# First inner-layer group split without waiting, sums moved behind emptied banks, in a two-layer hybrid decoder trunk

## The chip, the cores and the metric

One core of one Trainium2 chip runs the whole program. The metric is device time in microseconds (us) of one execution, the median of several. TensorE is called PE here, VectorE DVE, ScalarE ACT, GpSimd POOL; SP is the queue on which almost all DMAs are issued.

## The reference

256 tokens of width 1024 pass through two layers. Each layer has a block of token mixers and then a squared-ReLU MLP of inner width 4096; all that the change touches is the MLP:

```python
def squared_relu_mlp(h, w_up, w_down):
    return jnp.square(jax.nn.relu(h @ w_up)) @ w_down
...
    for l in range(DEPTH):
        ...
        h = rms_norm(x, mlp_norm[l])
        x = x + squared_relu_mlp(h, w_mlp_up[l], w_mlp_down[l])
    return rms_norm(x, final_norm)
```

Everything is float32, and the results are wanted at nearly float32 precision.

## The kernel before

**Three products for one.** Every float32 operand is split into a rounded part (`hi`, type fp32r) and the rest (`lo`). A product is three matmuls (`three`, lines 300 to 303): hi with hi, hi with lo, lo with hi. ACT makes `hi` by a copy, DVE makes `lo` by a subtraction. For a weight the copies are `whi<-raw` (L280) and `wlo<-raw,whi` (L282); for the inner activations they are `sq<-hturned` on ACT and on DVE (both L322).

**The stream of weights.** Weights come in pieces of 128 x 1024 floats, 512 KB, in the order of use. SP issues their DMAs (`raw<-wts`, L218) into 7 rotating `raw` buffers, and the split pieces go to 6 rotating `whi`/`wlo` pairs. A DMA can start when DVE has finished with the `raw` buffer that it overwrites, and a split when PE has finished with the pair that it overwrites. One piece is 12 matmuls for PE.

**The MLP.** `up(i)` multiplies by one piece of the first matrix, `down(i)` by one of the second. Four ups make a group `g` of 512 inner columns for 256 tokens, in two PSUM banks (`pup`, tag `misc`, four banks). `squared_relu(g)` then sends the group on a long way: ACT applies the relu (L1332) and squares (L1334), DVE transposes blocks of 32 (`hblocks`, L331), one DMA writes them to HBM (`bounce`, L343), four DMAs read them back so that the inner columns lie on the partitions (`hturned`, L347), and `h_ready(g)` splits the result into `sq` (L322). PE needs `sq` for the four downs of that group. The order of PE's work is written out by hand in `mlp_order`: ten ups first (`LEAD = 10`), then downs and ups in turn. So the first down of a layer comes six ups after the group that it needs is complete.

**Seven products for eight.** For the groups in `SEVEN`, 1, 2, 3, 4 and 6 of each layer, two of the four downs are replaced by `seven(f)`, a 2 x 2 block product with seven multiplications. It needs sums of blocks of the activations (`h_sums`: four DVE operations `hsum`, then a split into `sumhi`, `sumlo`) and sums of blocks of the weights (`wsum`, `raw<-wsum,raw`, each split likewise). Two of the seven products go into the two banks of the group `g + 2`, which are then added into SBUF tiles (`carried`, L1402). The next ups need these banks. The first time this is a copy, on ACT in the kernel before.

**What sets the order.** Instructions are recorded in program order and then ordered by a scheduler for each engine, except where the kernel pins them. Each engine works through its queue strictly in order. `behind[key]` lists instructions after which the DMA and the split of the weight `key` are to be placed, and `tc.issue_after(x)` places what follows after `x`. The list `order` holds the weights still to be fetched, so `order[4]` is the fifth from there. In the second layer DVE also makes `xblocks`, transposes of the residual stream, and SP issues the DMAs that belong to them (`xbounce`, `xtok`).

Of the kernel before, what the change touches and what calls it, by code (L numbers as in the profile page):

```python
# [21 lines left out]
NF = DFF // P  # L22
# [6 lines left out]
SEVEN = [(1, 2, 3, 4, 6)] * L  # L29
# [127 lines left out]
def trunk(ctx: ExitStack, tc: tile.TileContext, gx, wts, consts, gfin, gn, xtok, out):  # L157


    nc = tc.nc  # L160
# [166 lines left out]
    def blocks_tile(name):  # L327
        return sb.tile([P, 4 * S], F32, name=name + "blocks", tag="probT", bufs=2)
# [1 line left out]
    def turn_row(blocks, t, row):  # L330
        return nc.vector.transpose(blocks.rearrange("p (b j t e) -> p t j b e", b=4, j=4, t=2)[:, t], row)  # L331

    def turned_blocks(rows, name, tag, bufs):

        blocks = blocks_tile(name)
        for t in range(NT):
            turn_row(blocks, t, rows[t])
        return turned_by_hbm(blocks, name, tag, bufs)

    def turned_by_hbm(blocks, name, tag, bufs, last=None):  # L340

        bounce = dr.tile([P, 4 * S], F32, name="bounce", bufs=2)
        nc.sync.dma_start(bounce, blocks)  # L343
        turned = sb.tile([P, 4 * S], F32, name=name + "turned", tag=tag, bufs=bufs)
        for b in range(4):
            src = bounce.rearrange("(a p) (b r) -> b p a r", a=4, b=4)[b]
            dma = nc.sync.dma_start(turned[32 * b : 32 * b + 32, :].rearrange("p (a r) -> p a r", a=4), src)  # L347
        if last:
            behind.setdefault(last, []).append(dma)
        return turned  # L350
# [458 lines left out]
    def layer(l, xn, before):  # L809
# [219 lines left out]
        first = slot("mv", 3)  # L1029
# [28 lines left out]
        first = slot("gmoba1", 1)  # L1058
# [269 lines left out]
        def squared_relu(g):  # L1328

            rows = [w2k("relu") for _ in range(NT)]  # L1330
            for t in range(NT):
                relu = nc.scalar.activation(rows[t], us[g][t], AF.Relu, scale=xm.col[t])  # L1332
            for t in range(NT):
                nc.scalar.activation(rows[t], rows[t], AF.Square)  # L1334
            turned = turned_blocks(rows, "h", "t4", T4)
            if g + 1 < NF // 4:
                behind.setdefault(order[3 if g - 2 in SEVEN[l] else 4], []).append(relu)
            waiting[g] = turned
            if 0 < g < NF // 4 - 1:
                h_ready(g - 1, relu)  # L1340
            elif g:
                h_ready(g)

        waiting = {}

        def h_ready(g, after=None):

            turned = waiting.pop(g)
            sq = sb.tile([P, 2, 4, S], F32R, name="sq", tag=("Q", "KK")[g % 2], bufs=1)
            with ExitStack() as pinned:  # L1350
                if after:
                    pinned.enter_context(tc.issue_after(after.ins))
                latest[:] = split_turned(turned, [sq[:, i] for i in range(2)])
            for j in range(4):
                h2[4 * g + j] = sq[:, 0, j, :], sq[:, 1, j, :]
            if g in SEVEN[l]:
                sums[g] = h_sums(turned)

        sums, shared, carried = {}, [], []

# [13 lines left out]
        def seven(f):  # L1374

            g = f // 4
            first, final = g == SEVEN[l][0], g == SEVEN[l][-1]
            t1 = load_w(l, "down", f, 0)
            w11, t2, t3, t4, w21, w22 = load_w(l, "down", f + 1, 0)
            if first:  # L1380
                shared.extend(misc_tile(name) for name in ("pone", "pfive"))
                carried.extend(w2k("carried") for _ in range(NT))
            s1, s2, s2a, s3 = sums.pop(g)
            (a11, a12), a22 = ([tuple(h[:, :P] for h in h2[f + i]) for i in range(2)]), tuple(h[:, P:] for h in h2[f + 1])
            ends = dict(start=first, stop=final)
            middle = dict(start=False, stop=False)
            alone = dict(start=True, stop=True)
            moving = us.pop(g + 2, None) or [misc_tile("pend") for _ in range(NT)]
            for o, a, b, marks in (
                (shared[1], s1, t1, ends),  # L1390
                (accs[0], a12, w21, middle),
                (shared[0], a11, w11, ends),
                (accs[2], a22, t4, middle),
                (moving[1], s3, t3, alone),
                (moving[0], s2, t2, alone),
                (accs[1], s2a, w22, middle),
            ):
                three(o, *a, *b, **marks)
            emptied = []
            for i in (1, 0):  # L1400
                r, o = carried[i], moving[i]
                emptied.append(nc.scalar.copy(r, o) if first else nc.vector.tensor_add(r, r, o))  # L1402
            if final:
                shares()
            else:
                following = SEVEN[l][SEVEN[l].index(g) + 1]
                for key in (order[3], (l, "down", 4 * following + 2, 0)):
                    behind.setdefault(key, []).extend(emptied)

        def shares():  # L1410

# [34 lines left out]
        last = l == L - 1  # L1446
# [108 lines left out]
        for t in range(NT):  # L1555
            y = sb.tile([P, D], F32, name="y", tag="t4", bufs=T4)
            r = sb.tile([P, 1], F32, name="fr", tag="st", bufs=SMALL)
# [50 lines left out]
T4 = 8  # L1608
# [82 lines left out]
```

## Time and profile before

| quantity | value |
|---|---|
| median of the three runs | 813.55 us (813.05, 813.55, 817.36) |
| the profiled execution | 813.68 us |
| its span, first to last instruction | 811.8 us |
| mean granted clock of PE | 0.997 |
| PE busy | 800.5 us |
| DVE busy | 663.7 us |
| ACT busy | 480.3 us |
| read from and written to HBM | 168.81 MB, 18.87 MB |

A line of the timeline gives the start, the length, the engine, the line of the kernel, the operation, what it writes and reads, how many such in a row, and in brackets the idle time before it and what ended that. In the chain of waits each line is a start, a length and what the time went to; a DMA's length is that from its issue to its landing. The lines of the `windows` view give, for a stretch of time, the busy time of each engine and, after these, the granted PE clock. The lengths of the matmuls are modelled; their starts are recorded, so that the pace of PE is read from one start to the next.

### The profile page before, as it was taken

What the parts mean: (1) busy time and instruction counts of PE and PEld (TensorE: products, weight loads), DVE (VectorE), ACT (ScalarE), POOL (GpSimd) and SP (SyncE); (2) the same over time, 40 slices, a digit from 0 to 9 for tenths busy, and PEclk for the clock granted to TensorE, in tenths of its full rate; (3) what the DMA queues carried; (4) which work ended last, traced back from release to release, by engine and by line L of the source; (5) the groups of instructions that cost most, each with busy time, mean ns of one, the idle gap of its engine ahead of it and who ended that gap; (6) DMA issues with size and microseconds to landing.
All of it is one profiled execution on the core that took longest, in us unless ns stands there. A gap on an engine that the chain in (4) does not pass through costs nothing.

```text
span 811.8 us, 11411 instructions
## 1 busy us (share of the span) xinstructions
PE 800.5 (99%) x3921; PEld 666.5 (82%) x3921; DVE 663.7 (82%) x1128; ACT 480.3 (59%) x755; POOL 72.8 (9%) x63
## 2 busy tenths in 40 slices
PE   9999999999998999999999999999999999999997
PEld 7888887888887888888898888888888878788885
DVE  6869997978875878887797987698698757889786
ACT  7675664654565666666486566655545656666562
POOL 0100810000030000000025220000001200000000
PEclk9999999999999999999999999999999999999999
DMA  9975979965667767788647579689665587688851
GB/s 331 353 241 166 295 236 288 288 234 197 204 219 232 214 218 256 256 270 253 226 160 223 159 226 331 217 262 264 219 236 176 186 271 235 218 270 292 309 180 54
DMA packets 68122, 192.11 MB, mean 237 GB/s; under 512 B 8288, under 2 KB 25056, under 8 KB 67808
## 3 DMA queue, kind: packets, MB, share of 16 engines
q1 hardware_dynamic: 67488, 190.71, 72.4%
q8 instruction: 31, 0.51, 0.3%
q10 hardware_dynamic: 576, 0.67, 0.2%
q14 instruction: 27, 0.22, 0.1%
HBM read 168.81 MB, written 18.87 MB: 231 GB/s over the span
## 4 chain that ended last, share of the span: by engine, by line
PE 90%; DMA 3%; DVE 3%; ACT 1%; issue 1%; SPq 0%; POOL 0%; DVEq 0%; ACTq 0%
PE acc L301 17%; PE acc L303 17%; PE acc L302 16%; PE pup L301 6%; PE pup L302 6%; PE pup L303 6%; PE acc L1270 6%; PE acc L512 4%; PE acc L514 2%; DMA hturned<-bounce 1%; PE ps_s L1036 1%; DMA bounce<-hblocks 1%; DVE wlo L282 1%; PE acc L878 1%; PE po L675 1%; DMA raw<-wts 1%
## 5 line engine op out<-in xcount | busy, mean ns | idle before, releaser
L280 ACT ACTIVATE whi<-raw 128x1024 fp32r<-128x1024 f32 (+4 forms) x267 | 268.7, 1020 | 187.7 <-PE acc L303 107.5
L282 DVE TENSOR_TENSOR wlo<-raw,whi 128x1024 fp32r<-128x1024 f32 (+4 forms) x267 | 318.6, 1209 | 71.6 <-ACT whi L280 70.5
L301 PE MATMUL acc<-whi,xs 128*128 128x512 f32 (+1 forms) x304 | 119.4, 394 | 0.1
L302 PE MATMUL acc<-wlo,xs 128*128 128x512 f32 (+1 forms) x304 | 117.8, 388 | 0.0
L303 PE MATMUL acc<-whi,xs 128*128 128x512 f32 (+1 forms) x304 | 117.7, 388 | 0.0
L301 PE MATMUL pup<-whi,xs 128*128 128x512 f32 x256 | 99.8, 391 | 0.9 <-ACT carried L1402 0.9
L302 PE MATMUL pup<-wlo,xs 128*128 128x512 f32 x256 | 100.1, 391 | 0.0
L303 PE MATMUL pup<-whi,xs 128*128 128x512 f32 x256 | 99.7, 389 | 0.0
L301 PE MATMUL acc<-whi,sq 128*128 128x512 f32 x196 | 77.1, 394 | 2.0 <-ACT sq L322 2.0
L303 PE MATMUL acc<-whi,sq 128*128 128x512 f32 x196 | 77.0, 393 | 1.1 <-DVE sq L322 1.1
L302 PE MATMUL acc<-wlo,sq 128*128 128x512 f32 x196 | 76.8, 392 | 0.0
L301 PEld LDWEIGHTS acc<-whi,xs 128*128 128x128 f32 x304 | 57.0, 188 | 13.5 <-issue 0.8
L303 PEld LDWEIGHTS acc<-whi,xs 128*128 128x128 f32 x304 | 57.1, 188 | 11.4
L302 PEld LDWEIGHTS acc<-wlo,xs 128*128 128x128 f32 x304 | 57.1, 188 | 10.7
L301 PEld LDWEIGHTS pup<-whi,xs 128*128 128x128 f32 x256 | 48.1, 188 | 11.5 <-ACT carried L1402 1.3
L303 PEld LDWEIGHTS pup<-whi,xs 128*128 128x128 f32 x256 | 48.2, 188 | 10.1
L302 PEld LDWEIGHTS pup<-wlo,xs 128*128 128x128 f32 x256 | 48.2, 188 | 9.8
L603 ACT ACTIVATE prob<-prob,smx 128x128 f32<-128x128 f32 x64 | 28.3, 444 | 31.4 <-DVE smx L600 31.4
L388 POOL TENSOR_TENSOR sqsum<-sqsum,xsq 128x256 f32<-128x256 f32 x16 | 18.3, 1141 | 314.9 <-ACT xs L317 169.7
L301 PEld LDWEIGHTS acc<-whi,sq 128*128 128x128 f32 x196 | 36.9, 188 | 10.3 <-ACT sq L322 2.8
L303 PEld LDWEIGHTS acc<-whi,sq 128*128 128x128 f32 x196 | 37.1, 189 | 9.7 <-DVE sq L322 1.9
L302 PEld LDWEIGHTS acc<-wlo,sq 128*128 128x128 f32 x196 | 37.1, 189 | 7.7
(273 smaller groups left out, 1344.7 us busy)
## 6 DMA issues: line engine op xcount, KB each, us to landing
raw<-wts SPq DMA_DIRECT2D x264, 512.0 KB, 5.0
bounce<-hblocks SPq DMA_DIRECT2D x16, 512.0 KB, 4.5
hturned<-bounce SPq DMA_DIRECT2D x64, 128.0 KB, 3.7
pbounce<-blocks SPq DMA_DIRECT2D x8, 768.0 KB, 4.1
probT<-pbounce SPq DMA_DIRECT2D x32, 192.0 KB, 6.5
qkoth<-qkraw SPq DMA_DIRECT2D x48, 64.0 KB, 5.2
raw<-wts SPq DMA_DIRECT2D x5, 464.0 KB, 6.0
dec<-consts SPq DMA_DIRECT2D x2, 1024.0 KB, 7.0
```

The source lines that it names most:

```text
L280: fetched.append(nc.scalar.activation(hi[:, cs], raw[:, cs], AF.Copy))
L282: nc.vector.tensor_sub(lo[:, cs], raw[:, cs], hi[:, cs].bitcast(F32))
L301: nc.tensor.matmul(o, ah, bh, start=start, stop=False, **more)
L302: nc.tensor.matmul(o, ah, bl, start=False, stop=False, **more)
L303: nc.tensor.matmul(o, al, bh, start=False, stop=stop, **more)
L388: (nc.gpsimd if n < self.on_pool else nc.vector).tensor_add(self.sum, self.sum, sq)
L512: nc.tensor.matmul(acc, wh[:, k, :], xn.both(k), start=k == 0, stop=False)
L514: nc.tensor.matmul(acc[:, 0:S], wl[:, k, :], xn.k(k)[0], start=False, stop=k == KD - 1)
L603: nc.scalar.activation(p[:, a:b], p[:, a:b], AF.Exp, bias=m[:, 2 + i : 3 + i], scale=d**-0.5, accum_out=m[:, 4 + i : 5 + i])
L675: nc.tensor.matmul(dst, vh, pT[h + j][0], start=True, stop=False)
L878: nc.tensor.matmul(mq[n], wq[n][0], xn.both(k), start=k == 0, stop=False)
L1270: nc.tensor.matmul(o, a, b, start=half == 0 and i == 0, stop=4 * half + n == KD and i == len(jobs) - 1)
```

## The change

Five edits. First, `squared_relu(0)` of each layer calls `h_ready(0)` at once, where before the split of group 0 was made in `squared_relu(1)` and placed after the relu of group 1. Second, the weight of `down 4` is placed behind the last of the four reads of group 0. Third, for groups 0 to 2 no weight is placed behind the relu any more. Fourth, for a group in `SEVEN` whose predecessor is in it too (2, 3 and 4), the sums are no longer made in `h_ready` but at the end of the `seven` of the predecessor, after the last of the two instructions that empty its banks. Fifth, the first of these emptyings is a copy on DVE instead of ACT.

```diff
-    def turned_blocks(rows, name, tag, bufs):
+    def turned_blocks(rows, name, tag, bufs, last=None):
...
-        return turned_by_hbm(blocks, name, tag, bufs)
+        return turned_by_hbm(blocks, name, tag, bufs, last)
...
-            turned = turned_blocks(rows, "h", "t4", T4)
-            if g + 1 < NF // 4:
+            waiting[g] = turned_blocks(rows, "h", "t4", T4, None if g else (l, "down", 4, 0))
+            if SEVEN[l][0] <= g - 2 < NF // 4 - 3:
                 behind.setdefault(order[3 if g - 2 in SEVEN[l] else 4], []).append(relu)
-            waiting[g] = turned
-            if 0 < g < NF // 4 - 1:
+            if 1 < g < NF // 4 - 1:
                 h_ready(g - 1, relu)
-            elif g:
+            elif g != 1:
                 h_ready(g)
...
             if g in SEVEN[l]:
-                sums[g] = h_sums(turned)
+                if g - 1 in SEVEN[l]:
+                    waiting[g] = turned
+                else:
+                    sums[g] = h_sums(turned)
...
-                emptied.append(nc.scalar.copy(r, o) if first else nc.vector.tensor_add(r, r, o))
+                emptied.append(nc.vector.tensor_copy(r, o) if first else nc.vector.tensor_add(r, r, o))
...
+            if g + 1 in waiting and g + 1 in SEVEN[l]:
+                with tc.issue_after(emptied[-1].ins):
+                    sums[g + 1] = h_sums(waiting.pop(g + 1))
```

PE's own order is the same, matmul for matmul. On ACT, where the MLP begins (the same in both layers), the order before runs from the weight splits ahead of group 0's relu to group 0's split:

```order
L280 ACTIVATE whi<-raw 128x1024 x2
L1332 ACTIVATE relu<-pup,ms 128x512 x2
L280 ACTIVATE whi<-raw 128x1024
L1334 ACTIVATE relu<-relu 128x512 x2
L280 ACTIVATE whi<-raw 128x1024 x3
L1332 ACTIVATE relu<-pup,ms 128x512 x2
L280 ACTIVATE whi<-raw 128x1024
L1334 ACTIVATE relu<-relu 128x512 x2
L322 ACTIVATE sq<-hturned 128x1024
```

In this piece the first pair of relus is that of group 0, the second that of group 1. On ACT at the same place the order is now:

```order
L280 ACTIVATE whi<-raw 128x1024 x3
L1332 ACTIVATE relu<-pup,ms 128x512 x2
L1334 ACTIVATE relu<-relu 128x512 x2
L280 ACTIVATE whi<-raw 128x1024 x3
L322 ACTIVATE sq<-hturned 128x1024
L1332 ACTIVATE relu<-pup,ms 128x512 x2
L280 ACTIVATE whi<-raw 128x1024
L1334 ACTIVATE relu<-relu 128x512 x2
```

The weight split that stood between relu and squares has gone ahead of the relu, and group 0's split stands ahead of group 1's relu instead of behind its squares. On SP at the same place in the first layer, the difference between the two orders, minus for before and plus for now:

```order
 L343 DMA bounce<-hblocks 128x1024
+L218 DMA raw<-wts 128x1024
+L347 DMA hturned<-bounce 32x4x256 x4
+L218 DMA raw<-wts 128x1024 x3
+L343 DMA bounce<-hblocks 128x1024
 L218 DMA raw<-wts 128x1024 x2
 L347 DMA hturned<-bounce 32x4x256 x4
-L218 DMA raw<-wts 128x1024 x2
-L343 DMA bounce<-hblocks 128x1024
-L218 DMA raw<-wts 128x1024
-L347 DMA hturned<-bounce 32x4x256 x4
```

One weight, that of `down 4`, has moved from ahead of group 0's four reads to behind them, and one more weight stands ahead of group 1's reads. On DVE, in the second layer around the first `seven`, the order before from the weight sums ahead of group 2's split to the second half of group 3's block transposes:

```order
L241 TENSOR_TENSOR wsum<-raw 128x512 x2
L282 TENSOR_TENSOR wlo<-raw,whi 128x1024
L241 TENSOR_TENSOR wsum<-wsum,raw 128x512
L1367 TENSOR_TENSOR hsum<-hturned 128x128
L1368 TENSOR_TENSOR hsum<-hturned 128x128
L241 TENSOR_TENSOR raw<-wsum,raw 128x512
L1369 TENSOR_TENSOR hsum<-hsum,hturned 128x128
L322 TENSOR_TENSOR sq<-hturned,sq 128x1024
L1370 TENSOR_TENSOR hsum<-hsum,hturned 128x128
L331 STREAM_TRANSPOSE hblocks<-relu 128x4x4x32
```

Here the two copies `carried<-pup` are not in DVE's queue; they stand on ACT behind `sumhi<-hsum`. On DVE at the same place now, from group 2's split to the first two weight sums:

```order
L322 TENSOR_TENSOR sq<-hturned,sq 128x1024
L331 STREAM_TRANSPOSE hblocks<-relu 128x4x4x32
L1461 STREAM_TRANSPOSE xblocks<-GX 128x4x4x32
L1461 STREAM_TRANSPOSE xblocks<-x_70 128x4x4x32
L282 TENSOR_TENSOR wlo<-raw,whi 128x1024
L1404 COPY carried<-pup 128x512
L331 STREAM_TRANSPOSE hblocks<-relu 128x4x4x32
L1404 COPY carried<-pup 128x512
L1369 TENSOR_TENSOR hsum<-hturned 128x128
L1370 TENSOR_TENSOR hsum<-hturned 128x128
L241 TENSOR_TENSOR wsum<-raw 128x512 x2
```

The sums of group 2's activations and of the weights have moved behind the two copies, which are DVE's own now.

## The prediction

> **What bounds the kernel now.** I read the busy times first, then PE's waits, then the places where PE waited, and last the chain of waits that leads to each.
>
> ```profile
> span 811.8 us, 11411 instructions
> ...
> PE 800.5 (99%) x3921; PEld 666.5 (82%) x3921; DVE 663.7 (82%) x1128; ACT 480.3 (59%) x755; POOL 72.8 (9%) x63
> ```
>
> PE is busy in 99% of the span and does the same work after the change. So only time in which PE waits or runs slowly can be won. The view of PE's waits names three in the MLPs:
>
> ```profile
> PE acc L301 <- ACT sq L322: 2.0, 2, 1.5
> PE acc L303 <- DVE sq L322: 1.1, 2, 0.5
> PE pup L301 <- ACT carried L1402: 0.9, 1, 0.9
> ```
>
> Those are 4.0 us, but the columns (total, times, longest) do not hold all that a wait costs. In the first layer PE comes to group 0's first down at 256.7:
>
> ```profile
> 256.72 0.39 PE L303 MATMUL pup<-whi,xs 128*128 128x512 f32 x1
> 258.65 0.50 PE L301 MATMUL acc<-whi,sq 128*128 128x512 f32 x1 [1.54 <-ACT sq L322]
> ...
> 259.91 0.50 PE L303 MATMUL acc<-whi,sq 128*128 128x512 f32 x1 [0.52 <-DVE sq L322]
> ...
> 264.35 0.39 PE L303 MATMUL pup<-whi,xs 128*128 128x512 f32 x1
> 264.58 0.39 PE L301 MATMUL pup<-whi,xs 128*128 128x512 f32 x1
> ```
>
> At full pace one matmul follows another by 0.23 us (264.35 to 264.58). From 256.72 to 264.35 there are 15 steps, which should take 15 x 0.23 = 3.45 us and took 7.63: 4.2 us are lost, 2.06 in the two waits and most of the rest in the slow matmuls behind them. The stretches of the clock say why:
>
> ```profile
> 256.90:260.70 3.80, 1.74 (x6) 0.97 (x6) 2.07 (x2) 2.95 (x3) 0.00 (x0) 1.00 0.73 292
> 260.70:264.20 3.50, 3.50 (x10) 2.75 (x9) 1.43 (x2) 0.44 (x1) 0.00 (x0) 0.53 0.56 180
> ```
>
> After the waits the granted clock is 0.53 over 3.5 us, so 0.47 x 3.5 = 1.6 us go there. In the second layer the same place costs less, and the wait for `carried` comes in addition:
>
> ```profile
> 659.09 0.39 PE L303 MATMUL pup<-whi,xs 128*128 128x512 f32 x1
> ...
> 661.54 0.40 PE L301 MATMUL acc<-whi,sq 128*128 128x512 f32 x1
> ...
> 698.08 0.39 PE L303 MATMUL acc<-whi,sq 128*128 128x512 f32 x1
> 699.32 0.50 PE L301 MATMUL pup<-whi,xs 128*128 128x512 f32 x1 [0.86 <-ACT carried L1402]
> 699.66 0.39 PE L302 MATMUL pup<-wlo,xs 128*128 128x512 f32 x1
> ```
>
> Four steps from 659.09 to 661.54 took 2.45 instead of 0.92: 1.5 us. Two from 698.08 to 699.66 took 1.58 instead of 0.46: 1.1 us. So 4.2 + 1.5 + 1.1 = 6.8 us are what the change can win at these places.
>
> **Group 0: why it is late.** The chain of waits in the first layer:
>
> ```profile
> 241.31 1.27 ACT relu L1332 x2
> ...
> 243.56 1.07 DVE wlo L282
> ...
> 244.70 1.31 DVE hblocks L331 x2
> ...
> 246.03 3.88 DMA bounce<-hblocks
> ...
> 251.28 6.17 DMA hturned<-bounce
> ...
> 257.54 1.06 ACT sq L322
> ...
> 258.63 1.24 DVE sq L322
> ```
>
> ACT's split began when the last of the four reads landed, not when ACT was free. From its start to PE's first matmul are 258.65 - 257.54 = 1.11 us, and to the third, which needs DVE's part, 259.91 - 257.54 = 2.37. Without a wait PE would start these at 256.95 and 257.41. So ACT must start by 255.04 for PE not to wait at all: the split is 2.5 us late.
>
> *The weight split ahead of the relu.* It stood between relu and squares and held both ACT and DVE up.
>
> ```profile
> 237.84 1.06 ACT L280 ACTIVATE whi<-raw 128x1024 fp32r<-128x1024 f32 x1 [1.66 <-PE pup L303]
> ...
> 243.41 1.15 ACT L1334 ACTIVATE relu<-relu 128x512 f32<-128x512 f32 x2
> ```
>
> Weight splits wait for PE, which takes 12 x 0.23 = 2.76 us for a piece. So the next may start at 240.60 and end at 241.66. The relus then start 0.35 later than before and end at 242.93, the two squares end at 243.5 and 244.1, and DVE, done with the weight at 241.66 + 1.2 = 242.9, transposes each half as it comes, 0.65 each: the bounce is issued near 244.8 instead of 246.03, 1.2 us earlier.
>
> *One weight behind the reads.* SP's queue at this place, and from the view of the tile the landing times of all 64 such reads (least, median, greatest):
>
> ```profile
> 247.13 1.81 SPq L218 DMA_DIRECT2D raw<-wts  x2
> 249.96 1.75 SPq L347 DMA_DIRECT2D hturned<-bounce  x4
> ...
> DMA to landing us min/median/max: 2.6/3.7/6.2
> ```
>
> The reads waited for the bounce (246.03 + 3.88 = 249.91), not for SP. What the two weights cost them is the DMA engines: this group has the longest landing of all 64. Now one weight instead of two is issued between bounce and reads, some 2.5 us before them. With a bounce of 3.88 the reads start at 248.7, the last is issued 1.4 later (251.28 - 249.91) at 250.1, and it lands at 253.8 with the median, at 252.7 or 256.3 with the extremes. I take the median, because the greatest value belongs to the very case with two weights ahead. So ACT's split starts at 253.8, 1.2 us before it must. At 256.3 PE would wait 1.3 us.
>
> What this costs: SP is blocked until the bounce lands, and `down 4` is issued behind the reads, at about 250.5, up to 2 us later than before. PE uses it eight pieces after the first down, at 257 + 8 x 2.76 = 279, so that costs nothing. On ACT, group 0's split stands ahead of group 1's relus: they start at 254.9. Behind them is the fourth weight split after that at 240.60; PE frees its pair at 251.6 and, with six pairs, needs it five pieces later, at 265; it is done by 258. Group 1's own `sq` is due at `down 4`, 279; group 0 took 16.2 us from relu to split (241.31 to 257.54), so 254.9 + 16.2 + 2.4 = 273.5. Both are covered, the nearer one by 5 us. Further on SP, too, weights change places with reads; with seven buffers a weight has some 7 x 2.76 = 19 us from issue to use, against the 6 that the slowest read here took.
>
> In the second layer the same chain reads:
>
> ```profile
> 648.39 4.43 DMA bounce<-hblocks
> ...
> 654.20 4.53 DMA hturned<-bounce
> ```
>
> PE would start at 659.32 and 659.78, so ACT must start by 657.4. The bounce goes out 1.2 us earlier, at 647.2, lands at 651.6, the last read is issued 1.4 later at 653.0 and lands at 656.7 with the median, at 657.5 with this group's own 4.53. The first is in time, the second costs 0.1.
>
> [...] The granted clock fell here after two waits that add up to 2.06 us, and stayed full after the second layer's. [...]
>
> **The emptied banks.** In the second layer this is what held the copies back. On ACT the timeline has:
>
> ```profile
> 691.61 1.05 ACT L322 ACTIVATE sq<-hturned 128x1024 fp32r<-128x1024 f32 x1
> ...
> 698.16 0.63 ACT L227 ACTIVATE sumhi<-hsum 128x512 fp32r<-128x512 f32 x1 [3.52 <-DVE hsum L1370]
> ```
>
> On DVE at the same time stand:
>
> ```profile
> 691.83 0.69 DVE L241 TENSOR_TENSOR wsum<-raw 128x512 f32<-128x512 f32 x1 [3.93 <-DMA raw<-wts]
> ...
> 696.72 1.21 DVE L322 TENSOR_TENSOR sq<-hturned,sq 128x1024 fp32r<-128x1024 f32 x1
> 698.05 0.70 DVE L331 STREAM_TRANSPOSE hblocks<-relu 128x512 f32<-128x512 f32 x1
> ...
> 699.87 1.18 DVE L282 TENSOR_TENSOR wlo<-raw,whi 128x1024 fp32r<-128x1024 f32 x1
> ```
>
> DVE waited for a weight to sum, the activation sums came late, ACT waited for them, and the copies stood behind. Now sums stand behind the copies. DVE's part of `sq` can start when ACT's ends, 692.7; then come one `hblocks`, two `xblocks`, one `wlo`, a copy, the other `hblocks`, a copy. Two `hblocks` took 1.31 together and one 0.70, so DVE's operations overlap by some 0.08; an `xblocks` is the same transpose as an `hblocks`. So 692.7 + 1.13 + 3 x 0.62 + 1.10 = 696.8 for the start of the first copy. The trace has no DVE copy of a bank. Two rows bound it:
>
> ```profile
> L1402 DVE TENSOR_TENSOR carried<-carried,pup x12: 649/663/680, 317.0 to 761.4; 128x512 f32<-128x512 f32 x12
> L1402 ACT COPY carried<-pup x4: 567/580/590, 297.8 to 699.2; 128x512 f32<-128x512 f32 x4
> ```
>
> I take DVE's 0.66 rather than ACT's 0.58, since the engine and the bank are the same. The first copy is done at 697.5, the second at 698.7. PE wants the first bank at 698.08 + 0.23 = 698.3 and the second three matmuls later, 699.0. Neither waits, with 0.3 us to spare at the second. The first layer has no `xblocks` there and 1.2 us more.
>
> What is late next: the sums for the following `seven`, which starts here:
>
> ```profile
> 713.07 0.39 PE L301 MATMUL pfive<-sumhi 128*128 128x512 f32 x1
> ```
>
> Behind the copies stand, up to the last of these sums, seven `wlo` of 1.1, eight sums of 0.6 and four `hsum` of 0.2: 13.3 us, to 712.0. PE needs that last sum in the fifth product, four times three matmuls or 2.7 us later, at 715.8: 3.8 us of cover, and nothing is charged.
>
> The sum: 813.68 - 4.2 - 1.5 - 1.1 = 806.9 us. The profiled execution is 0.13 over the median and 1.9 over its own span.
>
> **The rivals.**
> - *The reads still land late.* SP sends three weights right behind them, and the DMA engines may be shared out as before. With 6.17 again PE waits 1.2 us in the first layer and, by the same slip of 1.6, about 1.5 in the second; half clock behind the first adds up to 1.6. Time 808.1 to 811.2. For: DMA ended both waits. Against: the median of 3.7.
> - *The half clock is not the waits'.* It would stay: 806.9 + 1.6 = 808.5. For: it begins when PE is already running again. Against: PE's clock is full before these waits, and 0.997 in the mean.
> - *Copies late on DVE.* The fuller engine (82%) takes them. If its `sq` comes 1 to 2 us later, PE waits 0.7 to 1.7 in the second layer, and up to 0.4 in the first, which has no `xblocks` there: 807.6 to 809.0; with half clock behind it 810.6.
> - *Slower: sums too late for the next `seven`.* They start only when the banks are empty, for three groups of each layer. If DVE is held there by a weight on its way, 3.93 us as above, plus 1.8 of other delay, PE waits 5.7 - 3.8 = 1.9 at each, and with 1.6 of half clock behind it 3.5: 806.9 + 6 x 3.5 = 828. It decides from 4.9 us of delay each, since 6 x 1.1 eats the gain. For: DVE is held like that once. Against: the same weights are then 4 us further on their way.
>
> **How the numbers follow.** 0.60 for the forecast, 0.14 for late reads, 0.05 for the clock, 0.11 for late copies, 0.10 for late sums. A measurement of this kernel can tell about 0.5%, 4.1 us of 813.55, from no change, so faster means under 809.5: the forecast (0.60), the clock (0.05), half of the late reads (0.07) and half of the late copies (0.05), 0.77. Slower is most of the late sums, 0.07, and 0.01 of the copies, together 0.08; the rest is 0.15. The range goes down to 805.9, the forecast less the 0.5 by which the lowest run lies under the median and less 0.5 for small waits that go along; it goes up to 810.0, which takes in the clock, most of the late copies and half of the late reads, and leaves out the late sums.
>
> **What would show it.** Right: PE without a wait for `sq` L322 at either group 0, `hturned` of group 0 landing within 4.5 us, the clock full through both MLPs, `carried<-pup` on DVE ending before PE's next `pup`. Wrong: waits of PE for `sumlo` or `sumhi`, or for the second copy, or a half-clock stretch in the MLPs without a wait ahead of it.

## The result, and the profile after

| | before | after |
|---|---|---|
| median, timed in turn on one chip | 815.28 us (813.05 to 817.36, 5 runs) | 807.53 us (805.86 to 807.80, 5 runs) |
| the profiled execution | 813.68 us | 807.37 us |
| its span | 811.8 us | 805.6 us |
| PE busy | 800.5 us | 797.5 us |

The ratio is 0.9906, 95% interval 0.9882 to 0.9929. The kernel is faster by 0.9% (0.7 to 1.2%), and 807.53 lies 0.6 us over the forecast. The view of PE's waits after the change:

```profile
PE warm L789 <- PEq L1689: 0.8, 1, 0.8
PE acc L512 <- ACT th L709: 0.8, 1, 0.8
PE acc L512 <- ACT c L822: 0.4, 1, 0.4
PE ps_s L1036 <- DVE KK L977: 0.2, 1, 0.2
```

No row of an MLP is left. The row with `th` is in the first layer's mixers, at 112.7 us, where the two programs are the same; the profiled execution of before did not have it. Because of it, and of 0.2 us at the start, PE reaches the first layer's MLP 1.07 us later than before (257.79 against 256.72), and every time of that MLP below is to be read with 1.07 taken off. From there to the end PE gains 6.2 + 1.07 = 7.3 us. In the timeline PE now goes from the tenth up into the first down at its full pace of 0.23:

```profile
257.79 0.39 PE L303 MATMUL pup<-whi,xs 128*128 128x512 f32 x1
258.01 0.39 PE L301 MATMUL acc<-whi,sq 128*128 128x512 f32 x1
258.24 0.39 PE L302 MATMUL acc<-wlo,sq 128*128 128x512 f32 x1
```

The stretches that held the waits and the half clock are full, with PE's busy time in the first column after the length and the clock in the sixth:

```profile
256.90:260.70 3.80, 3.80 (x18) 3.18 (x17) 2.92 (x5) 3.80 (x6) 0.00 (x0) 1.00 0.14 27
260.70:264.20 3.50, 3.50 (x17) 2.88 (x16) 3.14 (x3) 1.82 (x3) 0.00 (x0) 1.00 0.94 320
```

The way of group 0 on ACT, from the weight that went ahead to the split:

```profile
241.87 1.06 ACT L280 ACTIVATE whi<-raw 128x1024 fp32r<-128x1024 f32 x1 [1.91 <-PE pup L303]
242.84 1.25 ACT L1332 ACTIVATE relu<-pup,ms 128x512 f32<-128x512 f32 x2
243.97 1.15 ACT L1334 ACTIVATE relu<-relu 128x512 f32<-128x512 f32 x2
...
254.82 1.06 ACT L322 ACTIVATE sq<-hturned 128x1024 fp32r<-128x1024 f32 x1 [3.71 <-DMA hturned<-bounce]
255.79 1.25 ACT L1332 ACTIVATE relu<-pup,ms 128x512 f32<-128x512 f32 x2
```

And on SP, with the landing times of these four reads from the view of the tile:

```profile
245.97 0.33 SPq L343 DMA_DIRECT2D bounce<-hblocks  x1
247.36 0.33 SPq L218 DMA_DIRECT2D raw<-wts  x1
250.17 1.75 SPq L347 DMA_DIRECT2D hturned<-bounce  x4
```

```profile
DMA to landing us min/median/max: 2.8/3.1/3.2
```

The bounce goes out at 245.97 - 1.07 = 244.9 instead of 246.0, one weight follows it, the reads land 3.1 us after their issue instead of up to 6.2, and ACT's split starts at 253.75, 1.3 us before it must (255.04). In the second layer PE runs 3.26 us earlier than before (655.83 against 659.09), so that ACT's deadline of 657.4 lies at 654.1 here, and the split starts 1.1 us before it:

```profile
653.07 1.06 ACT L322 ACTIVATE sq<-hturned 128x1024 fp32r<-128x1024 f32 x1 [3.91 <-DMA hturned<-bounce]
```

On DVE at the first `seven` of the second layer the copies have taken the place that the prediction worked out; PE comes to the first bank at 693.46 and to the second three matmuls later, 694.14:

```profile
687.85 1.22 DVE L322 TENSOR_TENSOR sq<-hturned,sq 128x1024 fp32r<-128x1024 f32 x1 [2.07 <-ACT sq L322]
...
691.91 0.68 DVE L1404 COPY carried<-pup 128x512 f32<-128x512 f32 x1
692.51 0.70 DVE L331 STREAM_TRANSPOSE hblocks<-relu 128x512 f32<-128x512 f32 x1
693.13 0.65 DVE L1404 COPY carried<-pup 128x512 f32<-128x512 f32 x1
```

They are done 0.9 us and 0.4 us ahead of PE.

The forecast was worked out from one execution of 813.68 us. The medians, 815.28 and 807.53, lie 7.75 us apart, more than the 6.8 forecast.

### The profile page after: what moved, and what is told of

It reads as the page before. It is cut to its first block, busy times and chain, and to the rows that moved or that the text cites. A ratio compares the mean times of both kernels' runs of the same rounds, so it can differ in the third digit from the quotient of the medians.

```text
span 805.6 us, 11421 instructions
## 1 busy us (share of the span) xinstructions
PE 797.5 (99%) x3921; PEld 666.4 (83%) x3921; DVE 666.4 (83%) x1132; ACT 478.3 (59%) x751; POOL 72.4 (9%) x63
## 4 chain that ended last, share of the span: by engine, by line
PE 98%; ACT 1%; DVE 0%; issue 0%; DVEq 0%
PE acc L301 17%; PE acc L303 17%; PE acc L302 17%; PE pup L303 8%; PE pup L301 8%; PE pup L302 8%; PE acc L1270 6%; PE acc L512 4%; PE acc L514 2%; PE ps_s L1036 1%; PE acc L878 1%; PE po L675 1%; PE ps_s L581 1%; PE warm L789 0%; PE acc L880 0%; PE po L677 0%
```

## Experiments

Theory: the gain is made of three places that do not depend on one another, the first half of the change (edits 1 to 3, group 0) being worth 5.7 us of the forecast, and the second (edits 4 and 5, copies and sums) 1.1. Rival: the places hang together. Times are medians of the runs; kernels with the same "sitting" were timed on one chip in turn, and ratios are to the kernel before in that sitting.

### Sitting 1: the two halves

The changed kernel again:

> The changed kernel itself, timed beside its two halves. Theory (the three places gain independently): 6.5 to 8 us under the kernel before, at 805.9 to 807.8 us, PE without a wait in either MLP and no half-clock stretch in the middle. Rival (the difference came from how the first comparison fell, since the kernel before alone spread over 4.3 us): under 4 us of difference.

Measured: 808.28 us, ratio 0.9922 (0.9898 to 0.9945), 7.2 us under the kernel before's 815.52. In the profiled execution PE waited 0.8 us for `carried` in the second layer, of which the first profile had nothing:

```profile
PE pup L301 <- DVE carried L1404: 0.8, 2, 0.6
```

There group 2's split, and with it the whole chain to the copies, began 1.4 us late behind its reads. The place is right in the order but has little to spare.

The first half alone:

```diff
-                if g - 1 in SEVEN[l]:
-                    waiting[g] = turned
-                else:
-                    sums[g] = h_sums(turned)
+                sums[g] = h_sums(turned)
...
-                emptied.append(nc.vector.tensor_copy(r, o) if first else nc.vector.tensor_add(r, r, o))
+                emptied.append(nc.scalar.copy(r, o) if first else nc.vector.tensor_add(r, r, o))
...
-            if g + 1 in waiting and g + 1 in SEVEN[l]:
-                with tc.issue_after(emptied[-1].ins):
-                    sums[g + 1] = h_sums(waiting.pop(g + 1))
```

> Only the first three edits (split at once, down 4's weight behind the reads, no weight behind the first relus); copies on ACT and sums in h_ready as in the kernel before. Theory: the two group-0 places gain 4.2 + 1.5 = 5.7 us and the second layer's wait for carried stays (0.9 us wait, 1.1 us lost), so about 1.1 to 1.3 us slower than the whole change, some 808.7. Rival (the copies only came late because PE had been held at group 0, so that this half already removes that wait): as fast as the whole, within 0.3 us.

Measured: 819.88 us, ratio 1.0065 (1.0039 to 1.0090). Both views fall. This half does what it is meant to do at group 0, where PE no longer waits, and the kernel is 4.4 us slower than before it. Its waits:

```profile
PE pup L301 <- ACT carried L1401: 6.9, 2, 3.5
```

That is one wait of 3.5 in each layer, where the kernel before had 0.86 in the second alone. DVE, ACT and PE at the first of them:

```profile
290.32 0.69 DVE L241 TENSOR_TENSOR wsum<-raw 128x512 f32<-128x512 f32 x1 [4.43 <-DMA raw<-wts]
...
296.37 0.28 DVE L1369 TENSOR_TENSOR hsum<-hsum,hturned 128x128 f32<-128x128 f32 x1
```

```profile
296.69 0.63 ACT L227 ACTIVATE sumhi<-hsum 128x512 fp32r<-128x512 f32 x1 [6.03 <-DVE hsum L1369]
297.22 1.06 ACT L1401 COPY carried<-pup 128x512 f32<-128x512 f32 x2
```

```profile
294.00 0.39 PE L303 MATMUL acc<-whi,sq 128*128 128x512 f32 x1
297.84 0.50 PE L301 MATMUL pup<-whi,xs 128*128 128x512 f32 x1 [3.45 <-ACT carried L1401]
```

In the kernel before, the same weight sum and the same matmul of PE stand at:

```profile
290.94 0.69 DVE L241 TENSOR_TENSOR wsum<-raw 128x512 f32<-128x512 f32 x1 [2.72 <-DMA raw<-wts]
```

```profile
298.63 0.39 PE L301 MATMUL pup<-whi,xs 128*128 128x512 f32 x1
```

PE could have come at 294.23, 4.4 us earlier than before. DVE's weight sum came only 0.6 earlier, because it waits for a weight from HBM, and the chain from it through `hsum` and `sumhi` to the start of the copies took 6.9 us in both. In the kernel before this chain ended just ahead of PE: the two copies started at 297.85, and PE came at 298.63. In this layer the stall at group 0 had covered it; take the stall away and it is the next thing to be late. Behind the waits the clock falls to half, for one stretch of 3.41 us in the first layer and two in the second:

```profile
295.51:298.92 3.41, 1.08 (x5) 0.90 (x6) 3.41 (x5) 2.23 (x4) 0.00 (x0) 1.00 0.25 101
298.92:302.33 3.41, 3.41 (x10) 2.65 (x9) 3.41 (x5) 3.41 (x6) 0.00 (x0) 0.50 0.79 226
698.28:701.69 3.41, 0.53 (x3) 0.10 (x1) 3.41 (x9) 0.55 (x2) 0.00 (x0) 1.00 0.52 154
701.69:705.10 3.41, 2.80 (x7) 2.22 (x8) 3.41 (x6) 3.41 (x7) 0.00 (x0) 0.50 0.40 157
705.10:708.50 3.40, 3.40 (x10) 2.62 (x9) 3.40 (x5) 2.71 (x5) 0.00 (x0) 0.50 1.01 284
```

Half of PE's busy time in them is lost, 0.5 x (3.41 + 2.80 + 3.40) = 4.8 us. With the waits that is 6.9 + 4.8 = 11.7, against 11.6 between the medians of this kernel and the whole.

The second half alone:

```diff
-            waiting[g] = turned_blocks(rows, "h", "t4", T4, None if g else (l, "down", 4, 0))
-            if SEVEN[l][0] <= g - 2 < NF // 4 - 3:
+            waiting[g] = turned_blocks(rows, "h", "t4", T4)
+            if g + 1 < NF // 4:
...
-            if 1 < g < NF // 4 - 1:
+            if 0 < g < NF // 4 - 1:
...
-            elif g != 1:
+            elif g:
```

> Only the last two edits (copies on DVE, sums behind them); group 0 as in the kernel before. Theory: 1.1 to 1.3 us under the kernel before; PE waits again for sq L322 in both layers (about 2.06 and 1 us) and the half-clock stretch of 3.4 us behind the first is there, 5.7 us slower than the whole change. Rival (the half clock was the run's, not the waits'): no half-clock stretch in the first layer's MLP, 4.1 us slower than the whole.

Measured: 814.47 us, ratio 0.9990 (0.9968 to 1.0012), 6.2 us slower than the whole. The waits for `sq` are back and `carried` is gone:

```profile
PE acc L301 <- ACT sq L322: 2.6, 2, 1.9
PE acc L303 <- DVE sq L322: 1.3, 3, 0.5
```

The half clock is there too, but behind the second layer's stall, not the first's. The distance to the whole is near the 5.7 us that the theory had here, but the 1 us under the kernel before cannot be told from no change. So the halves alone give +0.65% and -0.1%, together they give -0.8%: the rival holds.

The whole without its third edit:

```diff
-            if SEVEN[l][0] <= g - 2 < NF // 4 - 3:
+            if g + 1 < NF // 4:
```

> The whole change without its third edit: a weight stands between relu and squares again, so the bounce goes out at about 246.0 instead of 244.8 (in the time frame of the kernel before), and ACT splits group 0 behind group 1's squares. One weight only stands between bounce and reads. Theory (the second weight ahead of the reads made them late): reads issued 249.9 to 251.3 land 3.1 to 3.7 later, at 254.4 to 255.0, ACT is free at 254.4 and must start by 255.04, so no wait in the first layer and 0 to 0.5 in the second: 0 to 0.5 us slower than the whole change. Rival (the 1.2 us on the way to the bounce counted): reads land 5 to 6 us after issue as before, ACT's split starts at 256.3 to 257.5, PE waits 1.3 to 2 us in the first layer with up to 1.6 of half clock: 2 to 5 us slower than the whole change.

Measured: 808.83 us, ratio 0.9923 (0.9898 to 0.9948), 0.55 us over the whole, which such intervals do not tell apart. With one weight ahead of them group 0's reads land early here, although the bounce goes out late; the landing times in the first layer of this run, and in the second half alone, which has two weights ahead:

```profile
DMA to landing us min/median/max: 2.6/3.0/3.1
```

```profile
DMA to landing us min/median/max: 4.2/4.5/5.0
```

In the first layer the theory holds: the weight behind the reads did the work at group 0, PE did not wait there, and the 1.2 us on the way to the bounce were margin. In the second layer the margin was missed. The waits of PE in this execution:

```profile
PE acc L303 <- DVE sq L322: 1.0, 2, 0.5
PE acc L301 <- ACT sq L322: 0.5, 1, 0.5
```

At the second layer's group 0 PE waited 0.52 and 0.53 us and lost 1.6 us (four steps from 657.23 to 659.73), where the theory had at most 0.5. The reads landed in 2.6 to 3.1 us there too, but behind a bounce that went out at 646.52 and took 5.9 us. The other wait of 0.4 us is late in the first layer's MLP.

### Sitting 2: which edit needs which

Edits 1 and 2 on the kernel before:

```diff
-            turned = turned_blocks(rows, "h", "t4", T4)
+            waiting[g] = turned_blocks(rows, "h", "t4", T4, None if g else (l, "down", 4, 0))
             if g + 1 < NF // 4:
                 behind.setdefault(order[3 if g - 2 in SEVEN[l] else 4], []).append(relu)
-            waiting[g] = turned
-            if 0 < g < NF // 4 - 1:
+            if 1 < g < NF // 4 - 1:
                 h_ready(g - 1, relu)
-            elif g:
+            elif g != 1:
                 h_ready(g)
```

> Edits 1 and 2 on the kernel before: down 4's weight goes behind group 0's reads, everything else (order of ACT and DVE, group 1's queue on SP, copies on ACT behind the sums) as before. Theory (the weights' own chain, not PE, sets when DVE's weight sums for the first seven can run, at about 290.5 to 294 in the first layer whether PE stalled at group 0 or not; a PE that comes 4 us earlier then waits for the copies behind them): PE waits 2.5 to 3.5 us for carried in both layers, and the time is between the kernel before and 5 us over it, like the first half alone. Rival (the third edit, which puts one more weight ahead of group 1's reads, is what made the copies late): wait for carried at most 1 us, time 4.5 to 6 us under the kernel before.

Measured: 811.42 us, ratio 0.9967 (0.9945 to 0.9990). The truth lies between the two:

```profile
PE pup L301 <- ACT carried L1401: 2.7, 2, 2.4
```

In the first layer, where PE's stall at group 0 is gone, the copies hold PE for 2.4 us without the third edit as well, so the cover that went with the stall is the cause there. In the second layer they hold it for 0.3 only, against 3.5 in the first half, which has the third edit too. Two things make up the difference. PE still lost 1.2 us at this layer's group 0 here, so that part of the cover was left; and DVE's weight sum came 31.83 us after PE's last up ahead of the first down here (691.15 against 659.32) and 33.75 us after it in the first half (694.77 against 661.02), 1.9 us later. What paces the weights ahead of that place was not tried.

The whole with the copies on ACT:

```diff
-                emptied.append(nc.vector.tensor_copy(r, o) if first else nc.vector.tensor_add(r, r, o))
+                emptied.append(nc.scalar.copy(r, o) if first else nc.vector.tensor_add(r, r, o))
```

> The whole change with the two copies on ACT again; they now stand ahead of the activation sums on ACT, since those stay behind the copies, while on DVE the weight sums are again ahead of group 2's split. Theory (the copies were late only because they stood on ACT behind sumhi, which waits for DVE's held-up sums): DVE waits some 4 us for the weight again, but PE does not wait for carried: as fast as the whole change, within 0.5 us. Rival (DVE held up for 4 us delays something that PE needs, its part of sq or sumlo): PE waits at least 1 us for DVE in one of the layers, 1.5 to 4 us slower than the whole.

Measured: 811.36 us, ratio 0.9975 (0.9955 to 0.9994). The copies are early, as the theory had it, and yet PE waits, as the rival had it, at another place than either thought:

```profile
PE pup L301 <- DVE carried L1404: 2.7, 2, 2.5
```

These are the additions at the second `seven` of the second layer. On DVE the weight sums are ahead of group 2's split again, and one waits:

```profile
689.54 0.69 DVE L241 TENSOR_TENSOR wsum<-raw 128x512 f32<-128x512 f32 x1 [4.57 <-DMA raw<-wts]
```

So group 3's bounce goes out at 698.75, where in the first profile of the whole it went at 693.23. Its reads, with two weights ahead of them, take up to 5.7 us, and the additions stand behind the split that waits for them. The chain of waits:

```profile
704.98 5.74 DMA hturned<-bounce
710.82 1.07 ACT sq L322
711.91 0.58 DVE sq L322
```

So the copies need not be on DVE to be early. What their place on DVE brings is that the weight sums are queued behind them, and no longer hold up what feeds the next group.

The whole with the activation sums at the split again:

```diff
-                if g - 1 in SEVEN[l]:
-                    waiting[g] = turned
-                else:
-                    sums[g] = h_sums(turned)
+                sums[g] = h_sums(turned)
...
-            if g + 1 in waiting and g + 1 in SEVEN[l]:
-                with tc.issue_after(emptied[-1].ins):
-                    sums[g + 1] = h_sums(waiting.pop(g + 1))
```

> The whole change with the activation sums of groups 2 and 3 made at their split as before, the copies on DVE. On DVE the four hsum stand ahead of sq and one sumlo ahead of the copies, 4 x 0.2 + 0.6 = 1.4 us more, and both copies stand behind the second hblocks, 0.6 more for the first. Weight sums stay behind the copies. Theory (the place behind the held-up weight sums was the costly one, not the activation sums): PE waits 0.5 to 1.9 us for carried in the second layer and up to 0.9 in the first, 0.5 to 3 us slower than the whole. Rival (making the activation sums early is what holds the copies, through sumhi): waits of 3 us and more as in the first half alone, 8 us or more slower than the whole.

Measured: 808.56 us, ratio 0.9944 (0.9920 to 0.9968).

```profile
PE pup L301 <- DVE carried L1401: 1.7, 2, 1.4
```

Together the waits are of the size expected, but the longer one, 1.4 us, is in the first layer, where at most 0.9 were. The theory holds: by the ratios (1.0065 for the first half, 0.9922 for the whole, 0.9944 here) most of the 11.6 us are won with the weight sums behind the copies. The place of the activation sums cost these 1.7 us of waits in the one execution with a trace.

The whole without its first edit:

```diff
-            if 1 < g < NF // 4 - 1:
+            if 0 < g < NF // 4 - 1:
...
-            elif g != 1:
+            elif g:
```

> The whole change without its first edit: group 0's split stands on ACT behind group 1's two relus instead of ahead of them (the relus end at about 254.4 in the time frame of the kernel before, PE needs the split to start by 255.04). Theory: the split starts 0.6 us later than in the whole change and PE does not wait for it in the first layer; same as the whole within 0.3 us. Rival (the split's place ahead of the relus is needed): PE waits at least 0.5 us for sq in one of the layers, 0.5 to 2 us slower.

Measured: 806.19 us (805.86 to 806.49, 6 runs), ratio 0.9904 (0.9885 to 0.9922), the lowest time of all, and PE is without a wait in either MLP. ACT's split starts at 253.94 behind group 1's relus, still when the reads land.

### Sitting 3: the first edit, and the price of a stall

The changed kernel again:

> The changed kernel once more, so that the version without the first edit is timed against it on one chip in one sitting. Both views expect 806 to 809 us.

And without its first edit:

> The whole change without its first edit, timed directly beside the whole. Theory (the first edit moves nothing that PE waits for; the 806.19 us of the first timing were the sitting): within 0.5 us of the whole. Rival (with the split behind group 1's relus, the relus and what hangs on them come sooner, and PE's rest of waits at the copies of the second layer goes): 1 to 2 us faster than the whole, and without the spread of 2.7 us.

Measured side by side: the whole 807.13 us, ratio 0.9900 (0.9867 to 0.9933); without the first edit 807.37, ratio 0.9903 (0.9866 to 0.9939). In the sitting before, the latter had 0.9904, so the 806.19 was the sitting. Placing group 0's split at once changes nothing that these runs can tell.

The trace of the whole holds something else. PE waits for `sq` twice in the first layer's MLP, once at group 0 (0.28 us) and once near the end (0.53), and the reads of group 0 land late, in the second view:

```profile
PE acc L303 <- DVE sq L322: 0.8, 2, 0.5
```

```profile
DMA to landing us min/median/max: 4.6/5.2/5.7
```

Only one weight stood ahead of these reads, as in the first profile of the whole, where they took 2.8 to 3.2 us. But the bounce had landed sooner (in 3.4 us against some 4.1), and the weight was under way for another 4.3 us when the first read was issued, against 1.7 there. So here it was not the number of weights that decided, but how long the last of them was still under way. The slack of 1.3 us at group 0 can be used up.

The last two kernels hold PE at group 0 by useless work on ACT. `h_ready` gets, ahead of the split, with one pair of lengths per layer:

```diff
+            for n in ((1,), (1, 1))[l] if g == 0 else ():
+                nc.scalar.activation(
+                    sq.rearrange("p two j s -> p two (j s)")[:, :n],
+                    turned[:, None, :].to_broadcast([P, n, 4 * S]),
+                    AF.Copy,
+                )
```

and group 1's relus are placed behind the split. The other kernel has ((1, 1), (2, 1)).

> The whole change with useless copies of hturned on ACT ahead of group 0's split (written where the split then writes), so that PE is held at the first down: in the first layer one copy and the weight split that slips in behind it, 2.1 us, less the 1.3 us of slack that the whole has there, so 0.85 us of stall; in the second layer two copies and one weight split, 3.2 less 1.1, so 2.1 us of stall. Theory (the clock is set for each 3.41 us slot of a fixed grid by what PE did in the slot before: idle for over some 1.7 us of it, half clock in the next): no half clock after the first, and after the second a slot of half clock in the executions in which 1.7 us of the stall fall into one slot, about 6 in 10; so 2.9 us over the whole in some executions and 4.6 in others. [...] Rival (the length of the stall decides, not the grid): half clock always after one of 2 us, 4.6 us over the whole each time.

Measured: 810.20 us (809.18 to 813.48, 12 runs), 3.1 us over the whole, ratio 0.9942 (0.9919 to 0.9966). In the profiled execution (810.80) PE lost 2.1 us at group 0 of the first layer and 1.8 in the second, and there was no half clock before the end of the program.

> The same with two copies in the first layer (1.9 us of stall) and a copy of double length, a single one and two weight splits in the second (5.3 less 1.1, so 4.2 us of stall, one stretch of 3.4 to 3.7 us at its start). Theory (grid of 3.41 us slots, idle for over some 1.7 us): half clock after the second stall in every execution for one slot, sometimes two, after the first in about half of them; 7.8 to 9.5 us over the whole. [...] In all cases the half clock begins and ends a whole number of 3.413 us after the clock first went up.

Measured: 815.75 us (812.09 to 821.04, 12 runs), 8.6 us over the whole, ratio 1.0006 (0.9980 to 1.0032). The profiled execution (813.00) has no half clock either, against the theory's "in every execution": its longest wait was 2.1 us, shorter than I had worked out, and PE lost 1.9 us in the first layer and 3.4 in the second. So the stalls were not the ones meant.

What sets the half clock is best seen over all traces. The records of the clock in a trace begin and end on a grid. In the kernel before it is full for 256.00 us, half for 3.41, full for 546.13: 75, 1 and 160 slots of 3.4133 (256.00 / 75). In the first profile of the whole it is full for 798.72 us, 234 slots. In the second half alone it is full for 655.36, 192 slots; in the first half for 293.55, 399.36 and 105.81, which are 86, 117 and 31. Here are two such slots and the one behind each, in the kernel before and in the last kernel. The table has all slots in the MLPs with PE busy for up to 2.1 us, a few above that, and some in which PE finishes its work at the end of the program.

```profile
257.49:260.90 3.41, 1.72 (x6) 1.15 (x7) 2.27 (x2) 2.95 (x3) 0.00 (x0) 1.00 0.66 266
260.90:264.31 3.41, 3.41 (x9) 2.65 (x9) 1.23 (x2) 0.55 (x1) 0.00 (x0) 0.50 0.61 190
```

```profile
656.63:660.04 3.41, 1.68 (x8) 1.06 (x6) 1.79 (x2) 3.41 (x4) 0.00 (x0) 1.00 0.18 23
660.04:663.45 3.41, 2.29 (x9) 1.57 (x10) 2.73 (x3) 3.41 (x6) 0.00 (x0) 1.00 0.68 223
```

| PE busy in the slot | kernel, place | clock in the next |
|---|---|---|
| 0.53 | first half, second layer | half |
| 0.94 | copies on ACT, second layer | half |
| 1.01 | edits 1 and 2, first layer | half |
| 1.02 | second half, second layer | half |
| 1.08 | first half, first layer | half |
| 1.72 | before, first layer | half |
| 1.68 | last kernel, second layer | full |
| 2.04 | sums at the split, first layer | full |
| 2.12, 2.14 | the kernel with the shorter useless work, first and second layer | full |
| 2.65, 2.88 | second half, first layer | full |
| 0.65, 1.24, 1.37 | end of the program: first half, copies on ACT, second half | half |
| 1.85, 1.91, 1.92, 2.29 | end of the program: last kernel, edits 1 and 2, the whole, before | full |

The border lies near 1.7, half a slot; the two values beside it stand the wrong way round by 0.04, for which the modelled ends of the matmuls may account. By this reading a stall of 2 us costs 1.7 us more or nothing, by where it falls on the grid. The grid stands differently in each execution: in the 14 traces the clock first goes up between 3.4 and 6.7 us after the start of the span (4.90 in the kernel before, 5.88 in the first profile of the whole). In the kernel before it was the first layer's waits of 1.54 and 0.52 us that half clock followed; in the second half alone it followed the second layer's of 1.86 and 0.53; in the last kernel 2.13 and 0.72 passed without.

Of the executions without a trace the mean granted clock is known. Among those with one, the nine without half clock before the end of the program have 0.998 or 0.999, the four with one slot of it 0.995 to 0.997, and the first half, with three, 0.992. Read by this, the two kernels with useless work do say something. The first has 0.996 in two of its 12 runs and 0.998 or more in the others. The second has 0.998 or more in three runs, of 812.1 to 813.6 us; 0.997 in one; and 0.990 to 0.995 in eight, of 815.0 to 821.0 us. So the same kernel meets half clock in some executions and not in others. The counts are not those that the theory gave (6 in 10, and every one), and the rival's "always" does not fit the first kernel; the mean does not tell behind which stall a slot came.

It also answers in part why the kernel before spreads over 8 to 10 us in a sitting and the whole over 1 to 3. All 17 runs of the whole have 0.998 or more. Of the 66 runs of the kernel before in the three sittings only 18 do, with medians of 812.4, 813.5 and 813.0 us, against 816.2, 814.6 and 816.1 us for the others. So the runs with half clock are 1 to 4 us slower there, the longer waits that bring it on included. The 18 still range from 808.9 to 815.8 us, and what makes that rest is open.

## Why the prediction was right, and where it was wrong

**Steps that held.** Each number in the time of the kernel before, forecast and measured: bounce 244.8 and 244.9; ACT's split 253.8 and 253.75; group 1's relus 254.9 and 254.7; in the second layer the bounce near 647.2 in both (644.01 + 3.26); the split when the reads land, 656.7, and 656.3; the first copy 696.8 and 691.91 + 4.85 = 696.76; its end 697.5 and 697.4, the second's 698.7 and 698.6; DVE's copy 0.66 and 0.65 to 0.68. The 4.85 is by how much PE runs earlier at that place (698.08 + 0.23 against 693.46). The reads of the first layer were issued 0.3 later than forecast and landed 0.6 sooner after their issue.

**The sum.** It said 6.8; PE gained 7.3 from the first down on. 4.2 came at group 0 of the first layer (1.07 + 3.26 = 4.3 up to the second layer's MLP), 1.5 at the second layer's (3.26 to 4.85, with 0.1 elsewhere) and 1.1 at its first `seven`, behind which PE runs 5.97 earlier (699.66 before, 693.69 after). The second `seven` there, with a small wait not charged in the prediction, brought 0.2. The 1.07 lost ahead of the MLPs, 0.8 of it the `th` wait in the mixers, took back more than what was over, so that this execution gained 6.2 us of span. That forecast and median agree to 0.6 us is in part luck: neither the `th` wait nor the second `seven` was in the sum.

**Signs.** In the first trace of the whole every sign that the prediction named is there. In the other two they are not all: 0.28 us of wait at group 0 with reads landing in up to 5.7 us in one, 0.8 us of wait for the copies in the other. The order was right, and the margins, forecast as 1.2 us at group 0 and 0.3 at the second copy, are used up in some executions.

**A reading that was wrong.** Group 0's reads in the first layer were not the slowest of the 64 in the kernel before. Those of the second layer's group 3 took 6.0 to 6.2 us, with a median of 6.2 against 5.7. They too had two weights ahead, so that the choice of the median stands. But what was credited to the number of weights is the time for which the last is still under way, as the reads of 4.6 to 5.7 us behind one weight showed.

**Half clock.** It went with the waits, as the sum had it, and the rival that it would stay (808.5) is out. Of the six half slots of the MLPs in the table two follow waits of 3.45 and 3.49 us, those of the first half; the other four follow waits of 2.5 us and less, so waits shorter than a slot were enough.

**What was read wrongly into the sum** is the price of the second half. "Two from 698.08 to 699.66 took 1.58 instead of 0.46: 1.1 us" is what the wait cost while PE was 5.7 us late, and as the loss at that place it held. It is not what edits 4 and 5 are worth: without them the rest of the change takes 11.6 us more and loses 4.4 us to the kernel before. The sum came out right because the whole was forecast with both halves in it: the places of the copies were worked out along DVE's queue as it would be, not by taking off what was there. But the paragraph "what is late next" looked only at the sums of the following `seven`, not at what the copies on ACT would have cost, and the expectations for the two halves took the parts of the sum for parts of the change, which they aren't.

**Credits that went to the wrong edit.** The weight split ahead of the relu was forecast to send the bounce out 1.2 us earlier, and it went out 1.1 earlier; without it the time is 0.55 us more, within the intervals, with PE losing 1.6 us in the second layer of the one execution with a trace. Added to the first two edits alone, the third makes the kernel slower, by the ratios 0.9967 and 1.0065. The split of group 0 ahead of group 1's relus was counted as a part of the gain there; it changes nothing measurable. The credit for "one weight behind the reads" was right: all kernels with the second edit have one weight there in the first layer, those without it two. No run leaves out the second edit alone, so whether the third would do without it is not shown.

## What to carry to other kernels

When a stall goes, follow every chain that ran beside it and ask which ended just ahead of the stalled engine: that one may be late next. Here it ended in copies that held PE for 3.5 us, because DVE, ahead of them, waited 4.4 us for a weight. Parts of a sum over places are not the worth of the edits at them; a half of a change can lose what the whole gains. On an engine that works strictly in order, as DVE did through that wait, put what waits for a DMA behind what another engine waits for.

## What the runs showed of the hardware

- The half clock came in slots of 3.413 us on a grid that ran through an execution, behind a slot in which PE was busy for less than about half of it (1.37 us and less: always; 1.85 and more at full clock: never; 1.68 and 1.72 beside the border). Each cost up to 1.7 us. In the first half alone, a slot at half clock that again held a wait (2.80 busy, 1.40 at full pace) was followed by another.
- Four reads of 128 KB behind 512 KB weights landed the later, the longer the last weight was still under way when the first read was issued. At group 0 of the first layer: 1.7 us more, 2.8 to 3.2 us to landing (the whole, one weight); 3.8 us, 4.2 to 5.0 (second half alone, two weights); 4.3 us, 4.6 to 5.7 (the whole in the third sitting, one weight); 4.4 us, 5.0 to 6.2 (the kernel before, two weights).
- DVE copied a bank of 128 x 512 from PSUM in 0.65 to 0.68 us, the time of its addition from there (0.65 to 0.68), where ACT took 0.57 to 0.59.
